# Log decays of the DeltaNet heads: products of fp32 numbers in two ranges of tiles, in place of four split float32r sets

## The chip, the cores and the metric

The kernel runs on one core of a Trainium2 chip. The metric is the device time of one execution in microseconds (us). Each core has a matrix engine (TensorE, in the rows PE for the products and PEld for the loading of their weights), a vector engine (VectorE, DVE), an engine for activation functions (ScalarE, ACT), GpSimd (POOL) and a queue engine (SyncE, SP) that issues most transfers. Every engine takes its instructions in a fixed order.

## What is computed

One layer of a diffusion backbone over 256 context tokens and 512 latent tokens of width 1024. A token mixer with two groups of four heads (HGRN2, a gated linear recurrence, and gated DeltaNet), both run forward and backward, is followed by a mixture of 16 experts. The change is in the DeltaNet heads. The reference, cut to what matters for it:

```python
def gated_delta_chunk_scan(q, k, v, beta, log_a, s0):
    ...
    cum = jnp.cumsum(log_a.astype(jnp.float32).reshape(b, h, n, DN_CHUNK), axis=-1)
    ...
    diff = cum[..., :, None] - cum[..., None, :]
    decay = jnp.where(incl, jnp.exp(jnp.where(incl, diff, 0.0)), 0.0)
    kk = jnp.einsum('bhntd,bhnsd->bhnts', kn, kn).astype(jnp.float32)
    a_mat = jnp.where(strict, bn[..., :, None] * kk * decay, 0.0) + jnp.eye(DN_CHUNK, dtype=jnp.float32)
    ...
    sol = lax.linalg.triangular_solve(a_mat, rhs, left_side=True, lower=True, unit_diagonal=True)
    ...
    qk = jnp.einsum('bhntd,bhnsd->bhnts', qn, kn) * decay.astype(dt)
    ...
```

`log_a` is one number for a token, a head and a direction. `decay[t, s]` is the exponential of the sum of the log decays of the tokens after s up to t. The lower triangle of a tile belongs to the forward direction and the upper one to the backward direction.

## The kernel before

The 768 tokens stand in NT = 6 tiles of 128. The kernel takes the sums of log decays from TensorE. For a head `h`, `dn_decay(h)` (L594) writes a tile of masks scaled by the log decay of each token (`seg`, tokens in partitions) and multiplies it with a constant triangle, so that entry (s, t) of the product is the sum of the log decays between s and t. One direction uses the masks `le` and `gt`, the other `ge` and `lt`; both add up into the same PSUM tile. ScalarE then takes the exponential (`E`), scales it by `beta` for either direction (`EB` and the scratch tile `bm`, L621), and VectorE puts the two triangles together (L622, COPY_PREDICATED). `E` and `EB` go to `dn_prep`: the products `pkk` (keys with keys, L668) are scaled by `EB`, and `pqk` (L675) by `E`. `dn_inv` inverts the 128x128 triangles by blocks, a long series of short steps on VectorE, ScalarE and TensorE, and writes `UF` and `UB`. `dn_scan` then runs over the six tiles, with `pks`, `px`, `po` and `pS` on TensorE between steps on VectorE and ScalarE.

Before the change the log decays `la` were split into a part `lah` that float32r holds and the rest `lal` (L513 to L515). The triangles had float32r copies (`gtr`, `ltr`, L518 and L519). For a head there are thus four sets (two directions, two parts). A set is six scalings on ScalarE (L612) and two products (L614), one of 256 columns into `pe{h}_0` and one of 512 columns into `pe{h}_2`. Each PSUM tile is complete only after the last of the four sets, and the two exponentials (L617) come after that. The buffer of `seg` exists once, so a set waits until the products of the set before have read it; the scratch tile `bm` uses the same buffer.

`dn_decay(0)` and `dn_decay(1)` are called ahead of the loop over heads; inside it `dn_decay(h + 2)` stands between the inverse of head `h + 1` and the HGRN2 head `h`. What fills TensorE meanwhile are the projections: `proj_cm` (L459 and L465: `hq0pl`, `hf_0pl`, `hf_1pl`, `dq1pl`, ..., for HGRN2 and DeltaNet), `proj_tm` (L859: values `hi0p`, gates `z10p`), each with a split of the raw weights (cast on ScalarE L393, e.g. `hq00h`, rest on VectorE L394, `hq00l`). The convolution over `qc`, `kc`, `vc` takes most of VectorE's time early on. The order in which each engine gets its instructions is decided by a scheduler with its own cost model when the program is built, and only nudged by priorities in the code; so a change in one function moves instructions of others. In the mixture of experts, each expert is a series of products `pg`, `pu` (L1546), `at`, `xt`, `py` (L1584) over weights that arrive by transfers and are split on ScalarE and VectorE.

## Time and profile before

| | us |
|---|---|
| three runs | 950.5, 952.97, 954.2 |
| median | 952.97 |
| profiled execution: time, span of the core | 949.7, 947.9 |
| mean granted TensorE clock of the profiled execution | 0.977 |
| busy in the span: PE, PEld, DVE, ACT | 876.5, 715.5, 711.0, 548.0 |

The span runs from the first to the last instruction of the core; 1.8 us of the execution's time lie around it. A busy time is the sum over the records of an engine; where two records overlap they count once. The granted clock is 1.00 at 2.4 GHz and 0.50 at 1.2 GHz.

### The profile page before, as it was taken

To read this page: it belongs to the slowest core of one execution; us is meant where nothing else is said; L and a number is where in the kernel's file an instruction comes from. 1 tells how busy PE (TensorE), PEld (TensorE's weight loads), DVE (VectorE), ACT (ScalarE), POOL (GpSimd) and SP (SyncE) were. 2 spreads that over 40 slices of the span, in tenths; PEclk is the share of its full clock that TensorE was granted. 3 is DMA by queue.
4 is the path that set the end of the run, shared out by engine and by line. 5 is a ranking of instruction groups with operands and counts; after the bars stand their busy time and mean duration, and the time that the engine had idled before them with its cause. 6 is when DMAs were issued, how large, how long until landed. Compare 5 with 4: busy or idle time off the path is not lost. (4 is left out here: it accounts for less than half of the span.)

```text
span 947.9 us, 20548 instructions
## 1 busy us (share of the span) xinstructions
PE 876.5 (92%) x8221; PEld 715.5 (75%) x8221; DVE 711.0 (75%) x1438; ACT 548.0 (58%) x1127; POOL 95.8 (10%) x106
## 2 busy tenths in 40 slices
PE   2999998979989999899998989899999999999994
PEld 1678887868878887787886968757888887777772
DVE  2687479745897679865585655868989988888986
ACT  4347753485258634932533333137888888788762
POOL 3231100000010000100000010111111111010011
PEclk9999998999979999999999989999999999999998
DMA  9920711200102111138219187669999999999745
GB/s 315 314 65 18 252 52 41 69 23 24 47 24 57 35 45 27 35 104 268 90 50 298 57 277 282 211 229 388 371 371 370 361 371 375 374 363 377 285 138 141
DMA packets 116237, 179.91 MB, mean 190 GB/s; under 512 B 10023, under 2 KB 49251, under 8 KB 116008
## 3 DMA queue, kind: packets, MB, share of 16 engines
q1 hardware_dynamic: 109272, 163.49, 50.7%
q0 software_dynamic: 6544, 14.71, 4.6%
q8 instruction: 66, 1.08, 0.5%
q10 hardware_dynamic: 320, 0.34, 0.1%
q14 instruction: 35, 0.29, 0.1%
HBM read 170.18 MB, written 16.27 MB: 197 GB/s over the span
## 5 line engine op out<-in xcount | busy, mean ns | idle before, releaser
L1422 DVE TENSOR_TENSOR lo<-w,hi 128x1024 fp32r<-128x1024 f32 x184 | 216.7, 1221 | 26.8 <-ACT hi L1417 25.0
L1417 ACT CAST hi<-w 128x1024 fp32r<-128x1024 f32 x184 | 186.0, 1050 | 21.7 <-PE pu L1546 9.6
L1584 PE MATMUL py<-lo,ah 128*128 128x512 f32 x128 | 51.6, 403 | 0.7
L1584 PE MATMUL py<-hi,ah 128*128 128x512 f32 x128 | 50.5, 396 | 0.0
L1584 PE MATMUL py<-hi,al 128*128 128x512 f32 x128 | 49.4, 396 | 0.3 <-DVE al L1576 0.3
L1546 PE MATMUL pg<-lo,xh 128*128 128x512 f32 x120 | 48.6, 405 | 0.0
L1546 PE MATMUL pu<-lo,xh 128*128 128x512 f32 x120 | 48.2, 402 | 0.2 <-DVE lo L1422 0.2
L1546 PE MATMUL pg<-hi,xh 128*128 128x512 f32 x120 | 47.5, 396 | 0.0
L1546 PE MATMUL pu<-hi,xl 128*128 128x512 f32 x120 | 47.4, 395 | 0.0
L1546 PE MATMUL pu<-hi,xh 128*128 128x512 f32 x120 | 47.4, 395 | 0.0
L1546 PE MATMUL pg<-hi,xl 128*128 128x512 f32 x120 | 47.4, 395 | 0.0
L1402 POOL DMA_INDIRECT y_d<-y,cl x15 | 17.6, 1173 | 132.9 <-ACT y L1588 119.7
L1584 PEld LDWEIGHTS py<-lo,ah 128*128 128x128 f32 x128 | 24.0, 188 | 8.7 <-DVE lo L1422 3.4
L941 DVE TENSOR_TENSOR KS<-KS,F 128x384 f32<-128x384 f32 x56 | 28.7, 553 | 2.1 <-ACT km L904 1.5
L1395 POOL DMA_INDIRECT xg<-t_d,cl x15 | 18.4, 1226 | 115.5 <-PE xt L1534 111.2
L814 DVE TENSOR_SCALAR vs<-px,bs 128x128 f32<-128x128 f32 x48 | 16.7, 348 | 16.8 <-PE px L812 16.4
L1584 PEld LDWEIGHTS py<-hi,ah 128*128 128x128 f32 x128 | 24.0, 188 | 6.4 <-ACT ah L1575 0.6
L1584 PEld LDWEIGHTS py<-hi,al 128*128 128x128 f32 x128 | 24.0, 188 | 6.1 <-DVE al L1576 0.8
L1546 PEld LDWEIGHTS pu<-lo,xh 128*128 128x128 f32 x120 | 22.5, 188 | 8.0 <-DVE lo L1422 2.9
L1006 PE MATMUL psm<-wm,cl 128*32 128x128 f32 x512 | 24.0, 280 | 4.9 <-DMA wm<-in_w_mod_dram 4.8
L1546 PEld LDWEIGHTS pu<-hi,xh 128*128 128x128 f32 x120 | 22.5, 188 | 5.4
L1546 PEld LDWEIGHTS pg<-hi,xh 128*128 128x128 f32 x120 | 22.5, 188 | 5.4
(1065 smaller groups left out, 2641.2 us busy)
## 6 DMA issues: line engine op xcount, KB each, us to landing
w<-in_w_gate_dram SPq DMA_DIRECT2D x32, 1024.0 KB, 16.0
w<-in_w_up_dram SPq DMA_DIRECT2D x32, 1024.0 KB, 15.0
w<-in_w_down_dram SPq DMA_DIRECT2D x32, 1024.0 KB, 15.2
wm<-in_w_mod_dram SPq DMA_DIRECT2D x64, 256.0 KB, 4.0
wm<-in_w_mod_dram SPq DMA_DIRECT2D x16, 512.0 KB, 8.5
y_d<-zt POOLq DMA_DIRECT2D x8, 512.0 KB, 6.9
wor<-in_w_out_dram SPq DMA_DIRECT2D x7, 512.0 KB, 4.9
xt<-in_x_dram SPq DMA_DIRECT2D x4, 512.0 KB, 11.7
```

The costliest lines, as they stand in the source:

```text
L814: nc.vector.tensor_scalar(vs, px[:, 0:P], bs[:, d, i:i + 1], None, op0=ALU.mult)
L941: nc.vector.tensor_mul(kh, kh, tt(d, 1 - d))
L1006: nc.tensor.matmul(ps[32 * c_:32 * c_ + 32, P * j:P * j + P], cl[:, kb, :], raw[:, P * c_:P * c_ + P], start=(kb == 0), stop=(kb == KB - 1))
L1395: return nc.gpsimd.indirect_dma_start(out=dst, out_offset=None, in_=t_d[:, :], in_offset=bass.IndirectOffsetOnAxis(ap=idx, axis=0), bounds ...
L1402: i_ = nc.gpsimd.indirect_dma_start(out=y_d[:, :], out_offset=bass.IndirectOffsetOnAxis(ap=idx, axis=0), in_=src, in_offset=None, bounds_c ...
L1417: nc.scalar.copy(hi, raw)
L1422: s.append(lo_on.tensor_sub(s[1], raw, s[0].bitcast(F32)))
L1546: a_pu[0] = nc.tensor.matmul(ps, m[:, kb, :], ww[:, k, :], start=(kb == 0 and n == 0), stop=(kb == KB - 1 and n == 2))
L1584: mm = nc.tensor.matmul(ps, m[:, k, :], ww[:, k % 2, :], start=(k == 0 and n == 0), stop=(k == 3 and n == 2))
```

## The change

The split of `la` and the float32r copies of the triangles go. The six tiles are worked in two ranges of three. A range has its own PSUM tile and its own `seg` tile (three tiles by two directions), six scalings of the unsplit `la`, six fp32 products of 128 columns straight with the constant triangles, and one exponential of 384 columns. The scalings by `beta` and the merge of the triangles stay as they were. In the new program the lines stand 10 lower before `dn_decay` and 13 lower after it: scalings L602, products L603, exponential L604, scalings by `beta` L608, merge L609.

```diff
-    lah = cp.tile([P, NT, 8], F32, name="lah")
-    lal = cp.tile([P, NT, 8], F32, name="lal")
-    lahr = grr[:, 256:256 + NT * 8].rearrange("p (i n) -> p i n", i=NT)
-    nc.vector.tensor_copy(lahr, la)
-    nc.vector.tensor_copy(lah, lahr.bitcast(F32))
-    nc.vector.tensor_sub(lal, la, lah)
-    gtr = cp.tile([P, P], F32R, name="gtr")
-    ltr = cp.tile([P, P], F32R, name="ltr")
-    nc.vector.tensor_copy(gtr, K("gt"))
-    nc.vector.tensor_copy(ltr, K("lt"))
...
-        rng = ((0, 2), (2, 4))
-        pe = [psI(f"pe{h}_{t0}") for t0, n in rng]
-        for d, m in ((0, "le"), (1, "ge")):
-            for a, l in ((0, lah), (1, lal)):
-                seg = dn.tile([P, NT, P], F32R, tag="seg", name=f"seg{h}_{d}_{a}")
-                for i in range(NT):
-                    nc.scalar.mul(seg[:, i, :], K(m), l[:, i, 4 * d + h:4 * d + h + 1])
-                for j, (t0, n) in enumerate(rng):
-                    nc.tensor.matmul(pe[j][:, 0:n * P], (gtr, ltr)[d], seg[:, t0:t0 + n, :],
-                                     start=(d == 0 and a == 0), stop=(d == 1 and a == 1))
-        for j, (t0, n) in enumerate(rng):
-            nc.scalar.activation(E[:, t0:t0 + n, :], pe[j][:, 0:n * P].rearrange("p (i t) -> p i t", i=n), AF.Exp)
+        n = NT // 2
+        for t0 in (0, n):
+            pe = psI(f"pe{h}_{t0}")
+            seg = dn.tile([P, n, 2, P], F32, tag="seg", name=f"seg{h}_{t0}")
+            for i in range(n):
+                for d, m in enumerate(("le", "ge")):
+                    nc.scalar.mul(seg[:, i, d, :], K(m), la[:, t0 + i, 4 * d + h:4 * d + h + 1])
+                    nc.tensor.matmul(pe[:, i * P:(i + 1) * P], K(("gt", "lt")[d]), seg[:, i, d, :], start=(d == 0), stop=(d == 1))
+            nc.scalar.activation(E[:, t0:t0 + n, :], pe[:, 0:n * P].rearrange("p (i t) -> p i t", i=n), AF.Exp)
```

The order on ScalarE around the decays of head 0, before. Between the second pair of sets and the exponentials stand the sigmoids of the HGRN2 projection `hf_0` (`F`, `KS`) and two casts of weights for DeltaNet head 1 (`dk10h`, `dk11h`); the row `ACT_TABLE_LOAD` fetches the table of another function.

```order
L874 ACTIVATE F_1049<-hf_0pl 128x512
L874 ACTIVATE KS_1048<-hf_0pl 128x512
L612 ACTIVATE seg_1_1_721<-cst,lal 128x128 x6
L393 CAST dk10h<-dk1r_1664 128x512
L393 CAST dk11h<-dk1r_1670 128x512
L875 ACTIVATE F_1049<-hf_0pc 128x256
L875 ACTIVATE KS_1048<-hf_0pc 128x256
L617 ACT_TABLE_LOAD
L617 ACTIVATE E_690<-pe_0_692 128x256
L621 ACTIVATE EB_691<-E_690,beta 128x128 x2
L617 ACTIVATE E_690<-pe_2_693 128x512
```

The same engine now, from the copy of the query projection `dq0pl` into the padded tile on. Before, that copy stood 13 rows ahead of the piece above.

```order
L544 COPY lpad_659<-dq0pl 128x8x64
L604 ACT_TABLE_LOAD
L604 ACTIVATE E_681<-pe_0_683 128x384
L602 ACTIVATE seg_3_699<-cst,la 128x128 x6
L608 ACTIVATE EB_682<-E_681,beta 128x128 x3
L974 COPY vp_846<-hi0p_975 128x256
L393 CAST hq00h<-hq0r_1031 128x512
L393 CAST hq01h<-hq0r_1037 128x512
L624 COPY kt_778<-pk_0_782 128x256
L604 ACTIVATE E_681<-pe_3_698 128x384
```

The exponentials have moved ahead of the casts `hq00h` and `hq01h`, which stood right behind that copy, and ahead of all sigmoids of `hf_0`.

The order on TensorE where head 0 is scanned (`px`, `pS`, `pks`) and the decays of head 1 are taken, before:

```order
L614 MATMUL pe_2_1608<-seg_0_0_1609,gtr 128x512
L834 MATMUL pS_0_0_1879<-vs_0_0_1877,kd_0_0_1880 128x128
L812 MATMUL px_0_1_1884<-vt_798,UB_674 128x128
L970 MATMUL hpk_3_0_2812<-cst,KS_1048 128x128
L614 MATMUL pe_0_1607<-seg_0_1_1618,gtr 128x256
L834 MATMUL pS_0_1_1888<-vs_0_1_1886,kd_0_1_1889 128x128
L807 MATMUL pks_1_0_1893<-S_0_1873,kc_746 128x128
L614 MATMUL pe_2_1608<-seg_0_1_1618,gtr 128x512
L974 MATMUL hpS_3_0_2816<-vp_865,kst_3_0_2814 128x128
```

And now:

```order
L603 MATMUL pe_3_1603<-seg_3_1604,cst 128x128
L623 MATMUL pk_0_2044<-cst,kc_1632 128x128 x2
L603 MATMUL pe_3_1603<-seg_3_1604,cst 128x128
L821 MATMUL pS_0_0_1850<-vs_0_0_1848,kd_0_0_1851 128x128
L799 MATMUL px_0_1_1855<-vt_779,UB_665 128x128
L603 MATMUL pe_3_1603<-seg_3_1604,cst 128x128 x4
L459 MATMUL hq1pl<-hlo,hq11h 128x512
L961 MATMUL hpS_2_0_2753<-vp_846,kst_2_0_2751 128x128
L949 MATMUL hpo_2_1_2757<-vp_846,hatt_2707 128x128
```

Before, no projection stood among the first steps of this scan. Now the projection `hq1pl` of HGRN2 head 1 runs between them. Further on in the new order, the inverse of head 1 and the scan that follows it have a stretch of about 150 TensorE entries without a projection.

## Rows read from the trace of the kernel before

**Rows 1.** The page, part 1: busy time, share of the span, records.

```profile
PE 876.5 (92%) x8221; PEld 715.5 (75%) x8221; DVE 711.0 (75%) x1438; ACT 548.0 (58%) x1127; POOL 95.8 (10%) x106
```

**Rows 2.** Busy time by stretch; last columns granted clock, DMA share, GB/s.

```profile
75.00:550.00 475.00, 447.39 (x6097) 380.57 (x6096) 338.61 (x893) 254.29 (x734) 24.00 (x28) 0.98 0.27 83
98.00:114.00 16.00, 16.00 (x95) 14.06 (x93) 4.12 (x7) 12.64 (x35) 0.22 (x1) 1.00 0.86 303
130.00:180.00 50.00, 45.12 (x825) 39.44 (x824) 49.23 (x122) 19.64 (x48) 0.00 (x0) 0.93 0.17 42
140.00:160.00 20.00, 15.62 (x342) 13.22 (x344) 19.96 (x51) 5.11 (x11) 0.00 (x0) 0.83 0.21 54
192.70:213.10 20.40, 15.47 (x96) 11.66 (x92) 10.22 (x30) 18.62 (x58) 0.00 (x0) 1.00 0.10 27
250.00:280.00 30.00, 26.19 (x592) 20.61 (x592) 29.55 (x88) 14.85 (x50) 2.51 (x2) 0.83 0.11 29
370.00:400.00 30.00, 24.40 (x175) 20.46 (x174) 27.43 (x66) 27.07 (x92) 3.46 (x3) 0.94 0.12 36
677.33:695.45 18.12, 18.12 (x86) 14.81 (x85) 16.46 (x17) 15.50 (x18) 2.77 (x2) 1.00 1.04 363
817.24:835.95 18.71, 18.58 (x85) 14.58 (x85) 16.39 (x17) 15.04 (x18) 2.02 (x2) 1.00 1.04 368
```

**Rows 3.** Groups by line and shape on ACT: busy, mean ns | idle before, releaser.

```profile
L612 ACT ACTIVATE seg<-cst,lah 128x128 fp32r<-128x128 f32 x48 | 15.3, 401 | 1.6 <-DVE lah L514 1.6
L612 ACT ACTIVATE seg<-cst,lal 128x128 fp32r<-128x128 f32 x48 | 15.1, 389 | 1.3 <-PE pe L614 1.3
L617 ACT ACT_TABLE_LOAD x4 | 5.1, 1283 | 0.1
```

**Rows 4.** Timeline of PE: start, length, instruction, [idle before, releaser].

```profile
94.56 0.28 PE L614 MATMUL pe<-seg,gtr 128*128 128x256 f32 x1
94.67 0.39 PE L459 MATMUL hq0pl<-hhi,hq01l 128*128 128x512 f32 x1
...
96.96 0.39 PE L614 MATMUL pe<-seg,gtr 128*128 128x512 f32 x1
97.19 0.40 PE L459 MATMUL hf_0pl<-hhi,hf_00h 128*128 128x512 f32 x1
...
133.21 1.06 PE L668 MATMUL pkk<-kc 128*128 128x128 f32 x8
134.20 0.34 PE L910 MATMUL pa<-QP,km 128*32 128x32 f32 x16
134.46 1.16 PE L675 MATMUL pqk<-qc,kc 128*128 128x128 f32 x8
135.55 0.34 PE L910 MATMUL pa<-QP,km 128*32 128x32 f32 x16
```

**Rows 5.** Timeline of ACT, decays of head 0.

```profile
81.88 1.87 ACT L612 ACTIVATE seg<-cst,lah 128x128 fp32r<-128x128 f32 x6 [1.61 <-DVE lah L514]
...
88.32 0.59 ACT L554 COPY lpad<-dq0pl 128x512 f32<-128x512 f32 x1 [0.76 <-DVE vc L576]
...
107.01 0.36 ACT L875 ACTIVATE KS<-hf_0pc 128x256 f32<-128x256 f32 x1
107.40 1.28 ACT L617 ACT_TABLE_LOAD   x1
108.69 0.39 ACT L617 ACTIVATE E<-pe 128x256 f32<-128x256 f32 x1
```

**Rows 6.** Timeline of DVE: the merge of head 0.

```profile
114.11 1.03 DVE L622 COPY_PREDICATED EB<-cst,bm 128x768 f32<-128x768 int32 x1 [6.47 <-ACT bm L621]
```

**Rows 7.** Timeline of PE: three of its waits.

```profile
91.66 0.50 PE L459 MATMUL hq0pl<-hhi,hq00l 128*128 128x512 f32 x1 [0.74 <-DVE hq00l L394]
...
213.13 0.50 PE L459 MATMUL hf_1pl<-hhi,hf_10h 128*128 128x512 f32 x1 [1.75 <-ACT KS L874]
...
375.14 0.47 PE L614 MATMUL pe<-seg,gtr 128*128 128x512 f32 x1 [1.75 <-DVE UB L791]
```

## The prediction

> **What bounds the kernel now.** I began with the busy times of the page [rows 1]. TensorE is busy for 92% of the span and no other engine for more than 75%. A mean over the whole program hides the stages, so I cut the span into stretches [rows 2]. In the mixer, from 75 to 550 us, TensorE is busy for 447.4 of 475 us. Of the 27.6 us in which it is not, I looked for the stretches that hold most, and for what the other engines do there. The reader should see four kinds of place:
>
> - 98 to 114 us: TensorE is full (16.00 of 16 us) and VectorE is almost empty (4.12 us). The merge of head 0's decays ends that emptiness; it starts at 114.11 us, after VectorE waited 6.47 us for ScalarE [rows 6].
> - 130 to 180 us: VectorE is full (49.23 of 50 us) with head 0's inverse and scan, the HGRN2 head and the convolutions of head 1. TensorE idles 4.9 us, and its granted clock is 0.93. The core of it is 140 to 160 us: 4.4 us idle and a clock of 0.83, so part of it ran at 1.2 GHz.
> - 192.7 to 213.1 us: the scan of head 0 beside the decays of head 1, with no projection but one product. TensorE is busy for 15.47 of 20.4 us, ScalarE for 18.62 us.
> - 250 to 280 us and 370 to 400 us, the same for heads 2 and 3: TensorE idles 3.8 and 5.6 us; VectorE is busy 29.55 and 27.43 of 30 us; ScalarE is at 14.85 and 27.07 us.
>
> So the mixer is bound by TensorE, with holes where chains of short steps lack something to fill them. The decays lie ahead of the inverse, which opens these chains. In the experts, TensorE is full or nearly so (18.12 of 18.12 us, 18.58 of 18.71 us [rows 2]).
>
> **TensorE: what the change adds.** Removed are 4 heads x 4 sets x 2 products: 16 of 256 columns and 16 of 512. What one takes is the distance from its start to the next: 94.67 - 94.56 = 0.11 us and 97.19 - 96.96 = 0.23 us [rows 4]; together 16 x 0.34 = 5.4 us. Added are 4 x 12 = 48 fp32 products of 128 columns. The nearest rows are `pkk` and `pqk`, fp32 products of the same shape: four in 134.20 - 133.21 = 0.99 us, and four in 135.55 - 134.46 = 1.09 us (eight records, two for one product) [rows 4]. That is 0.25 to 0.27 us each, 11.9 to 13.1 us in all. TensorE gets 6.5 to 7.7 us more; I take 6.9, or 1.7 for a head. Heads 1 and 3 have their decays in stretches where TensorE idles, and pay little. For heads 0 and 2 TensorE is full around them, and I count all of it: **+3.4**. If the cover at heads 1 and 3 is gone, it is 6.9.
>
> **ScalarE: what it loses.** 96 scalings become 48. A run of six takes 1.87 us [rows 5], so one costs 0.31 us and not the 0.40 us of the group's mean [rows 3], in which neighbours overlap. 48 x 0.31 = 14.9 us. Exponentials are eight before and after, over the same columns: nothing. The new order has 21 table loads instead of 19, since the two exponentials of head 1 have other functions between them: 2 x 1.28 [rows 3] = 2.6 us. Net ScalarE has 12.3 us less.
>
> A table load takes 1.28 us, and around the one at 107.40 us the neighbours follow at once: KS ends at 107.37, the exponential begins at 108.69 [rows 5]. The Trainium skill ("ScalarE: Activation LUTs", "What ACT_TABLE_LOAD costs") gives a drain of about 1.38 us on top, 2.66 us for each switch; by it the two loads would cost 5.3 us of ScalarE instead of 2.6. In this trace no such gap stands.
>
> **VectorE** loses five copies and subtractions on small tiles. They lie between operations of the convolution. Only one is seen to be waited for: the first `seg` waited 1.61 us for `lah` [rows 5]. I count nothing for it, since TensorE has the projection `hi0p` at that time; at most it is a gain of 1.6 us.
>
> **Head 0: the decays come earlier.** In the new order the first exponential stands right behind the copy of `dq0pl`, which ends at 88.32 + 0.59 = 88.9 us [rows 5]. With its table load it starts at about 90.2, against 108.69. The second six scalings end at about 92.6, their products about 1 us later, and the second exponential at about 95. Twelve scalings by `beta` (12 x 0.31 = 3.7 us), the casts and a few squares of head 0's keys that stand between them bring the merge to about 101 us, 13 us earlier than 114.1 [rows 6]. It moves into the stretch in which VectorE has 12 of 16 us free [rows 2]. Then the scaling by `EB` and the inverse begin earlier, and 130 to 180 us, where VectorE is full, is relieved of part of them. What is there to win is the idle 4.9 us and the clock: 0.17 x 20 = 3.4 us of granted cycles from 140 to 160 us. That makes 8.3 at most. VectorE's work itself does not shrink, so the other end is nothing. I take **-5**, nearer the full end since 13 us are more than the hole is long.
>
> The cost of it: the cast `hq00h` stood right behind that copy and now stands behind a table load, an exponential (0.5 us), six scalings (1.87) and three by `beta`: about 4.7 us later. TensorE already waited 0.74 us for its rest `hq00l` [rows 7]. It now has the longer products of both ranges ahead (counted above) and transposes of keys and values, about 4 us, so the new wait would be 0.5 to 2.5 us, with the products of the second range pacing behind their scalings. I take **+1.5**.
>
> **Head 1: 192.7 to 213.1 us.** ScalarE is at 18.62 of 20.4 us. Twelve scalings fewer free 3.7 us, two more table loads take 2.6 back. The decays of head 1 now lie among products of `hq1pl`, which can run while a step waits, where before no projection stood. To win are 4.9 us by the busy time of TensorE. In the new order, though, a later piece (inverse of head 1 and the next scan) has lost its projections, and may idle in its place. I take **-3**, between 0 and -4.9.
>
> The weight loads are busy for only 11.66 us in that stretch [rows 2], so by them there are 8.7 us of room. The Trainium skill ("Perfetto Trace Analysis", "Identifying the Most-Contended Engine") holds that matmul busy time is a poor measure of headroom and points to the weight loads instead. By it the term could reach -8.7, and the sum would be up to 5.7 us lower. The trace has no row that decides this.
>
> **Heads 2 and 3.** The decays of head 2 lie beside a VectorE that is full (29.55 of 30 us): shorter scalings on a ScalarE with 14.85 us of work free nobody directly. Idle time there is 3.8 us; I take **-2**. At head 3 ScalarE is busy 27.07 of 30 us, and TensorE idles 5.6 us; a product waits 1.75 us there for the inverse [rows 7]. 3.7 us of ScalarE go: **-3.5**, between 0 and -5.6.
>
> **The experts.** They come in two forms, of 18.12 and 18.71 us [rows 2]; the second has a wait for a split weight in it. Six experts have the second order before, four in the new one: 2 x 0.6 = **-1.2**. The transfers of weights wait for buffers that the splits free, so I let the experts shift with the end of the mixer.
>
> **Sum.** 3.4 + 1.5 - 5 - 3 - 2 - 3.5 - 1.2 = -9.8 us against the profiled execution's 949.7: 939.9. That execution lies 3.3 us under the median of 952.97, so the median would be 943.2; I say **943.5**. With gains at their full ends (8.3 + 4.9 + 3.8 + 5.6 + 1.2 = 23.8) and costs at the low ones (3.4 + 0.5) it is -19.9: 933. With no gain and all costs (7.7 + 2.5) it is +10.2: 963.
>
> **Rivals.** A measurement of this kernel can tell about 0.5%, or 4.8 us, from no change; that puts "no change" at 948.2 to 957.7.
>
> *Holes only move.* VectorE's chain, not ScalarE, sets the length of the holes (49.23 of 50 and 29.55 of 30 us busy). Earlier decays let projections be used up earlier, and the next scan lacks them: the stretch without projections in the new order speaks for it. Against it: VectorE's free 12 us at 98 to 114 us are real room. The gains would be about 6 us instead of 14.7, against 4.9 of costs: -1, some 952.
>
> *TensorE pays (slower).* A kernel that is 92% TensorE gets 6.9 us more work for it, and relief of an engine at 58% is worth nothing. It needs head 1 and head 3 to lose their cover, and the waits at `hq00l` in full: 6.9 + 2.5 = 9.4 us. It ends slower by over 0.5% as soon as less than 9.4 - 4.8 = 4.6 us of holes are closed; with 2 us it is +7.4, or 960.
>
> *All holes close.* If head 0's start 13 us earlier takes the whole chain of heads along, the full gains stand: 933 to 936. Against it speaks that the chain of VectorE has as much work as before.
>
> **How the numbers follow.** My forecast 0.56 (937 to 950; some 0.07 of it above 948.2), all holes close 0.08, holes only move 0.20 (948 to 955, with 0.02 past either edge), TensorE pays 0.16. Faster: 0.49 + 0.08 + 0.02 = 0.59. Same: 0.07 + 0.16 = 0.23. Slower: 0.16 + 0.02 = 0.18. The range 931 to 960 leaves out half of the slower case and the edge of the fastest. The forecast's own range is 937 to 950.
>
> **What would show it.** Right: the first exponential of head 0 at about 90 us and its merge near 101; a TensorE group of 48 fp32 products at 0.25 to 0.27 us of pace; ScalarE's total down by about 12 us; less idle time and a clock near 1.00 at 140 to 160 us; four experts of the longer form. Wrong: the wait for `hq00l` over 3 us; a new hole of more than 5 us in the inverse of head 1 or the next scan; the end of the mixer no earlier although the merge is; products of the new form above 0.3 us, or at half clock, since they come in runs behind waits.

## The result and the profile after

The change makes the kernel faster by about 1%: 942.63 us median of four runs (939.4 to 945.5) against 952.75 us of four runs of the kernel before (950.5 to 954.2), a ratio of 0.9896 with a 95% interval of 0.9873 to 0.9920. The forecast was 943.5. The total came out as forecast, in part by luck: two effects behind the mixer that no term of mine had, one of about 5 us and one of 4 to 6 us, have opposite signs. Not all of the terms came out either. The experiments below show both.

First the page of the kernel after, part 1, and its groups for the lines of the change (these answer to [rows 1] and [rows 3]):

```profile
PE 868.5 (92%) x8285; PEld 719.7 (77%) x8285; DVE 712.9 (76%) x1433; ACT 536.4 (57%) x1081; POOL 99.2 (11%) x106
```

```profile
L602 ACT ACTIVATE seg<-cst,la 128x128 f32<-128x128 f32 x48 | 15.0, 391 | 2.4 <-DVE EB L609 1.6 <-DVE la L509 0.8
L604 ACT ACT_TABLE_LOAD x5 | 6.4, 1283 | 0.1
L604 ACT ACTIVATE E<-pe 128x384 f32<-128x384 f32 x8 | 3.9, 489 | 0.9 <-PE pe L603 0.9
```

ScalarE is busy 11.6 us less (548.0 to 536.4); I had worked out 12.3. TensorE is busy 8 us less (876.5 to 868.5) although it was given more products; where that comes from is said below (the clock, and the pace of the experts).

The decays of head 0, on ScalarE, VectorE and TensorE (compare [rows 5], [rows 6] and the first of [rows 7]):

```profile
86.57 0.59 ACT L544 COPY lpad<-dq0pl 128x512 f32<-128x512 f32 x1 [0.76 <-DVE vc L566]
87.18 1.28 ACT L604 ACT_TABLE_LOAD   x1
88.47 0.49 ACT L604 ACTIVATE E<-pe 128x384 f32<-128x384 f32 x1
88.86 1.85 ACT L602 ACTIVATE seg<-cst,la 128x128 f32<-128x128 f32 x6
...
91.75 0.62 ACT L393 CAST hq00h<-hq0r 128x512 fp32r<-128x512 f32 x1
```

```profile
97.90 1.09 DVE L609 COPY_PREDICATED EB<-cst,bm 128x768 f32<-128x768 int32 x1 [1.36 <-ACT bm L608]
```

```profile
84.41 1.50 PE L603 MATMUL pe<-seg,cst 128*128 128x128 f32 x12
85.67 0.36 PE L846 MATMUL hi0p<-hi01l,hhi 128*128 128x256 f32 x1
...
93.84 0.48 PE L459 MATMUL hq0pl<-hhi,hq00l 128*128 128x512 f32 x1
```

The first exponential starts at 88.5 us instead of 108.7, the merge at 97.9 instead of 114.1, and the first product with `hq00l` at 93.84 instead of 91.66. The idle time of 0.74 us that stood before this product [rows 7] is gone: its row has none.

The stretches (columns as in [rows 2]; the first row here is the kernel before, from 75 us to the first product of the output projection, `mt`, which ends the mixer; the other rows are of after):

```profile
75.00:539.00 464.00, 436.39 (x6037) 371.36 (x6036) 329.38 (x875) 245.68 (x710) 22.95 (x27) 0.98 0.27 80
```

```profile
75.00:527.60 452.60, 431.60 (x6098) 373.17 (x6097) 330.17 (x870) 234.73 (x664) 25.56 (x27) 0.99 0.28 82
140.00:160.00 20.00, 18.26 (x428) 15.68 (x419) 20.00 (x53) 8.26 (x20) 0.00 (x0) 1.00 0.22 56
192.70:213.10 20.40, 18.43 (x346) 15.90 (x346) 15.62 (x56) 9.97 (x37) 1.33 (x1) 1.00 0.10 27
169.00:187.00 18.00, 18.00 (x137) 16.14 (x136) 12.56 (x23) 16.74 (x43) 0.00 (x0) 1.00 0.28 74
250.00:280.00 30.00, 26.04 (x226) 21.96 (x225) 28.54 (x77) 20.88 (x73) 3.98 (x3) 0.94 0.14 36
360.00:390.00 30.00, 25.88 (x311) 23.91 (x310) 25.48 (x62) 23.31 (x71) 5.92 (x3) 0.89 0.15 44
713.10:730.90 17.80, 17.80 (x86) 14.79 (x85) 16.42 (x17) 15.39 (x19) 2.84 (x2) 1.00 1.01 380
```

From 140 to 160 us the idle time fell from 4.4 to 1.7 us and the granted clock rose from 0.83 to 1.00. A stretch is the same time in both kernels, not always the same work. The decays of head 1, whose products stood at 192.8 to 202.6 us, now have theirs at 171.7 to 179.9 us, and TensorE does not idle around them (18.00 of 18 us busy). What stands at 192.7 to 213.1 us now idles for 2.0 us, where it was 4.9. Around 250 to 280 us a hole is still there (4.0 us idle, clock 0.94), and so is one at 360 to 390 us, where the decays of head 3 lie (4.1 us idle, clock 0.89). The mixer ends 11.5 us earlier (`mt` at 527.58 us, before at 539.04), with 21.0 us of idle time in place of 27.6. The clock adds to it: some 0.02 x 464 = 9 us of granted cycles missing before, 0.01 x 453 = 5 us now.

Two things happen behind the mixer that no term of mine had. An expert runs in 17.80 us where the same sequence of products took 18.12 before [rows 2]. And some of the 11.5 us are lost at once at the first expert. Timeline of after there, TensorE, then ScalarE, then SyncE's queue:

```profile
629.07 1.09 PE L1521 MATMUL xt<-cst,xg 128*128 128x128 f32 x8 [2.93 <-DMA xg<-t_d,cl]
634.88 1.11 PE L1554 MATMUL at<-cst,a 128*128 128x128 f32 x4 [4.72 <-DVE a L1545]
```

```profile
632.22 1.28 ACT L1544 ACT_TABLE_LOAD   x1 [14.61 <-SPq L1448]
```

```profile
618.44 1.23 SPq L1206 DMA_DIRECT2D w<-in_w_gate_dram  x2
621.03 0.37 SPq L1206 DMA_DIRECT2D w<-in_w_down_dram  x1
632.59 0.38 SPq L1206 DMA_DIRECT2D w<-in_w_up_dram  x1
```

L1448 is the branch on the overflow of experts. ScalarE comes to it early, then stands until SyncE's queue is done there, and only then takes the first expert's activation `a`, for which the transposes `at` wait. The instructions of the two queues at that line (count, ns, first and last start):

```profile
L1448 ACTq COMPARE_BRANCH  x1: 45/45/45, 614.0 to 614.0; - x1
L1448 SPq COMPARE_BRANCH  x1: 50/50/50, 621.4 to 621.4; - x1
L1448 SPq EVENT_SEMAPHORE  x8: 17/17/17, 626.9 to 632.1; - x8
```

In the kernel before, the last to come there was TensorE's own queue:

```profile
637.98 1.28 ACT L1557 ACT_TABLE_LOAD   x1 [10.56 <-PEq L1461]
```

The new order has four loads of weights ahead of the branch on SyncE's queue instead of two. In the trace three of them stand between the reading of the count and the branch (the SyncE rows above up to 621.03 us), where the kernel before has one. SyncE takes its compare at 621.4 us, so it is not the wait for free buffers that holds it. It then waits at the branch for each of its transfers: in the trace the second of the three loads has landed at 629.09 us and the third at 631.75, and SyncE's waits for these two end at 629.11 and 631.77. In the kernel before the one load has landed at 635.22 us and SyncE is through at 635.8, ahead of TensorE's queue. TensorE then starts the next expert after a pause in which its clock falls; from 634.9 to 643.5 us it is full but granted 0.68 (products 0.43 us apart at first, 0.23 later):

```profile
634.90:643.50 8.60, 8.60 (x29) 7.01 (x30) 4.40 (x6) 3.92 (x5) 0.00 (x0) 0.68 0.99 358
```

So `at` is only 5.8 us earlier than before (640.65 to 634.88), and the end of the program 7.9 us in the profiled executions (947.9 and 940.0 us).

### The profile page after: what moved, and what is told of

Read it like the earlier page. It is cut to its first block, busy times and chain, and to the rows that moved or that the text cites. A ratio compares the mean times of both kernels' runs of the same rounds, so it can differ in the third digit from the quotient of the medians.

```text
span 940.0 us, 20633 instructions
## 1 busy us (share of the span) xinstructions
PE 868.5 (92%) x8285; PEld 719.7 (77%) x8285; DVE 712.9 (76%) x1433; ACT 536.4 (57%) x1081; POOL 99.2 (11%) x106
## 5 line engine op out<-in xcount | busy, mean ns | idle before, releaser
L1031 POOL TENSOR_TENSOR nss<-nss,half 128x4 f32<-128x4 f32 x8 | 10.6, 1326 | 202.0 <-DVE nss L1028 125.2
```

The lines of the kernel that those rows point to most:

```text
L1031: nc.gpsimd.tensor_tensor(ss, ss, half[:, 0:NLT], op=ALU.pow)
```

## The experiments

Twelve kernels were run. A table first. "Mixer's end" is the start of `mt`; idle and clock of TensorE are those of the stretch from 75 us to it; the merge is that of head 0; all from one profile each. The median and the ratio are of the timed runs against the kernel before on the same chip.

| kernel | median us | ratio, 95% interval | mixer's end | idle | clock | merge |
|---|---|---|---|---|---|---|
| before | 952.75 | | 539.0 | 27.6 | 0.98 | 114.1 |
| the change | 942.63 | 0.9896, 0.9873 to 0.9920 | 527.6 | 21.0 | 0.99 | 97.9 |
| fp32_old_layout | 951.37 | 0.9987, 0.9962 to 1.0011 | 540.3 | 28.6 | 0.97 | 105.3 |
| split_two_ranges | 958.94 | 1.0064, 1.0035 to 1.0092 | 547.6 | 34.2 | 0.96 | 110.8 |
| new_head0 | 949.45 | 0.9974, 0.9950 to 0.9998 | 535.5 | 24.7 | 0.98 | 97.6 |
| new_heads123 | 959.64 | 1.0105, 1.0053 to 1.0157 | 548.4 | 33.3 | 0.96 | 113.0 |
| before_head0_four_tiles | 954.26 | 1.0031, 1.0013 to 1.0048 | 542.6 | 34.1 | 0.97 | 102.2 |
| after_head0_late | 940.89 | 0.9898, 0.9867 to 0.9928 | 533.8 | 23.5 | 0.97 | 101.7 |
| after_two_loads_ahead | 937.23 | 0.9855, 0.9828 to 0.9881 | 526.5 | 20.2 | 0.99 | 97.1 |
| after_double_scalings | 962.18 | 1.0093, 1.0061 to 1.0124 | 550.8 | 31.8 | 0.96 | 106.9 |
| after_tiles_moved_back | 948.45 | 0.9992, 0.9961 to 1.0022 | 527.8 | 21.0 | 0.99 | 98.0 |
| after_tiles_512_up | 943.09 | 0.9913, 0.9884 to 0.9942 | 528.8 | 22.8 | 0.99 | 98.2 |
| after_products_twice | 942.16 | 0.9904, 0.9876 to 0.9932 | 531.7 | 15.4 | 0.99 | 99.5 |
| before_directions_swapped | 953.56 | 1.0010, 0.9988 to 1.0032 | 545.4 | 29.5 | 0.97 | 115.3 |

Four kernels of the table (the change, two loads, moved back, 512 up) have the same order in the mixer. Their mixers end at 526.5 to 528.8 us, so these four profiles agree within 2.3 us. That is no bound for one profile: the executions of one kernel spread further (the kernel before from 949.0 to 959.6 us in 25 runs), and some profiles are of a short or a long one.

The totals also hold what comes behind the mixer, and there the kernels are of two kinds. In the change, fp32_old_layout, after_double_scalings, after_products_twice and the two with moved tiles, three loads stand between the count and the branch; in the others it is one. And an expert takes 17.8 us where the four removed tiles are gone (moved back excepted), 18.1 us where they are kept. So the mixer's end says more on the decays than the median does.

**fp32_old_layout: the new products, without the two ranges.**

```diff
+        for d, m in ((0, "le"), (1, "ge")):
+            seg = dn.tile([P, NT, P], F32, tag="seg", name=f"seg{h}_{d}")
+            for i in range(NT):
+                nc.scalar.mul(seg[:, i, :], K(m), la[:, i, 4 * d + h:4 * d + h + 1])
+            for j, (t0, n) in enumerate(rng):
+                nc.tensor.matmul(pe[j][:, 0:n * P], K(("gt", "lt")[d]), seg[:, t0:t0 + n, :], start=(d == 0), stop=(d == 1))
...
```

> The fp32 products and the halved scalings of the change, but in the layout of before: one set of six scalings for a direction over all six tiles, products of 256 and 512 columns, both exponentials only after the second set. Theory (my prediction's): the gain comes from decays that are ready earlier and from ScalarE's lighter load around them; ScalarE's part stays, the early exponential of the first three tiles goes, so some two thirds of the change's gain of 10 us, 944 to 948 us, and a merge of head 0 some 5 us later than with the change. Rival 1 (the split into two ranges does it): 951 to 955. Rival 2 (it is only where the fillers happen to be put): anything between 940 and 960, without relation to the merge of head 0.

Measured 951.4 us, no measurable gain. ScalarE has the lighter load (237.8 us to the mixer's end, before 245.7), and the merge of head 0 is 9 us earlier than before; but the mixer ends no earlier, although the hole at 140 to 160 us is closed. Halved scalings and the unsplit product together are worth nothing that can be seen in this layout.

```profile
75.00:540.30 465.30, 436.75 (x6034) 371.73 (x6033) 330.77 (x871) 237.80 (x666) 23.98 (x27) 0.97 0.27 80
140.00:160.00 20.00, 19.45 (x486) 17.01 (x474) 19.96 (x51) 6.73 (x15) 0.00 (x0) 1.00 0.22 56
```

**split_two_ranges: the two ranges, without the new products.**

```diff
+        for t0 in (0, n):
...
+            for d, m in ((0, "le"), (1, "ge")):
...
+                for a, l in ((0, lah), (1, lal)):
+                    for i in range(n):
+                        nc.scalar.mul(seg[:, a, i, :], K(m), l[:, t0 + i, 4 * d + h:4 * d + h + 1])
+                    nc.tensor.matmul(pe[:, 0:n * P], (gtr, ltr)[d], seg[:, a], start=(d == 0 and a == 0), stop=(d == 1 and a == 1))
```

> The two ranges of three tiles of the change, but with split float32r sets as before: 96 scalings, 32 products of 384 columns, no more work for TensorE than before. Theory (earlier decays and lighter ScalarE): the first range is ready after 12 scalings instead of 24, but ScalarE keeps its load: a small gain, 948 to 952 us. Rival 1 (the two ranges do it): the gain of the change plus the TensorE time that is not added, 937 to 943. Rival 2 (fillers by chance): 940 to 960.

Measured 958.9 us, slower than before. The merge of head 0 is only 3 us earlier than before, and the hole of the kernel before is still there:

```profile
140.00:160.00 20.00, 15.53 (x383) 12.76 (x384) 19.96 (x50) 5.10 (x11) 0.00 (x0) 0.83 0.22 55
```

With the former run it makes a square. Mixer's end: split sets in the old layout 539.0, fp32 in the old layout 540.3, split in two ranges 547.6, fp32 in two ranges 527.6 us. Each half alone gives nothing or costs 9 us; both together give 11.5.

**new_head0 and new_heads123: the change at some heads only.** Both keep the split parts and the old sets for the other heads.

```diff
+        if h == 0:
+            n = NT // 2
+            for t0 in (0, n):
...
+        else:
+            rng = ((0, 2), (2, 4))
...
```

In the second the condition is `h > 0`.

> The change at head 0 alone, heads 1 to 3 with split sets as before. My prediction's terms for it: +1.7 for products, +1.5 for the later cast, -5 for the earlier inverse, so -1.8 us: 951 us, with the hole at 140 to 160 us smaller. From the trace of the changed kernel, where the same work stands 1.5 us later at 110 us, 8 us earlier at 160 and 2 us earlier at 190, the same. Rival (head 0's start 13 us earlier takes the whole chain along): -6 to -10, 943 to 947. Rival (fillers by chance): 946 to 960.

> The change at heads 1 to 3, head 0 with split sets as before. My prediction's terms: -3 at head 1, -2 + 1.7 at head 2, -3.5 at head 3: -6.8 us, 946 us, if the heads' gains add up, and if the order of the experts stays that of before. Rival (TensorE pays where its cover is gone: 3 x 1.7 us): 955 to 958. Rival (fillers by chance): the two part runs do not add up to the whole, by more than 5 us.

Head 0 alone: 949.5 us, -2.5; my terms for head 0 gave -1.8. Heads 1 to 3 alone: 959.6 us, +7.7, where my terms gave -6.8. The parts add up to +5, the whole is -10 (at the mixer's end -3.5 and +9.3 against -11.5). What a head's new decays are worth depends on what the others did to the order. The rows of new_heads123 show where it loses: from the end of head 0's scan into head 1's, and where the scan of head 2 begins and the decays of head 3 end. The clock falls there too (in the kernel before, the same times have 4.0 and 3.3 us of idle time and clocks of 0.90 and 1.00):

```profile
250.00:300.00 50.00, 42.93 (x576) 37.73 (x575) 41.33 (x107) 31.64 (x104) 3.63 (x3) 0.83 0.09 23
380.00:410.00 30.00, 23.91 (x166) 22.06 (x166) 24.05 (x55) 21.13 (x63) 2.91 (x3) 0.89 0.09 27
```

**before_head0_four_tiles: early decays at head 0 by another way.**

```diff
-                seg = dn.tile([P, NT, P], F32R, tag="seg", name=f"seg{h}_{d}_{a}")
+                tag = ("seg", "vt", "kt", "vt")[2 * d + a] if h == 0 else "seg"
+                seg = dn.tile([P, NT, P], F32R, tag=tag, name=f"seg{h}_{d}_{a}", bufs=1 if tag == "seg" else 2)
```

> The kernel before, with one thing changed: at head 0 the four split sets take four tiles (three of them borrowed from buffers that are idle then), so that no set waits for the products of the set before. No new form of product, no lighter ScalarE. In the new order the first exponential of head 0 stands ahead of the casts of the HGRN2 weights, as with the change. Theory (the gain comes from head 0's decays being ready early, by whatever way): merge of head 0 near 100 us instead of 114, and a gain like that of the change at head 0 alone (-2.5 us there): 947 to 951. If moreover the early start of the scan is what the whole change lives on: 940 to 946. Rival (it is the unsplit products and the halved scalings): no gain, 951 to 955.

Measured 954.3 us: no gain, though the merge is at 102.2 us. The rows show that the mechanism worked and what it cost:

```profile
85.00:100.00 15.00, 9.93 (x55) 8.83 (x54) 5.64 (x10) 14.82 (x35) 2.57 (x5) 0.77 0.06 18
140.00:160.00 20.00, 18.47 (x449) 15.46 (x447) 20.00 (x52) 7.33 (x15) 0.00 (x0) 1.00 0.27 69
```

The hole at 140 to 160 us is closed (1.5 us idle, clock 1.00). But all 24 scalings now stand in one piece ahead of the work that feeds TensorE, which idles 5.1 of 15 us with a clock of 0.77 (before: 1.0 us and 1.00). With half as many scalings the change has its early merge without this price. The early merge does close the hole; that it carries the whole gain is refuted.

The whole table bears out both. In the ten kernels whose merge comes at 106.9 us or earlier, the clock at 140 to 160 us is 1.00 and the idle time at most 2.2 us; in the four with a merge at 110.8 us or later it is 0.83 and at least 4.4 us. But among the ten is after_double_scalings, the slowest kernel of all:

```profile
140.00:160.00 20.00, 19.97 (x456) 17.11 (x454) 20.00 (x53) 7.25 (x15) 0.00 (x0) 1.00 0.28 71
```

**after_head0_late: the change, with head 0's exponentials later.**

```diff
+            if h == 0:
+                tc.add_manual_dep(ex_.ins, conv_end[2].ins.name, later, reason="after the convolution")
...
-    dec[0] = dn_decay(0)
     with tc.issue_after(last_hi.ins):
         proj[0] = dn_proj(0)
+    dec[0] = dn_decay(0)
```

(`conv_end[2]` is the last step of the convolution of the queries. Unlike what the expectation says, one thing more is edited: the call of the decays of head 0 moves behind that of its projections.)

> The changed kernel, with the exponentials of head 0 put behind the convolution of the queries in the order, so that the merge of head 0 comes some 6 to 8 us later than with the change; nothing else is edited. Theory (head 0's early merge carries the gain): the gain is mostly lost, 948 to 954 us, and the hole at 140 to 160 us comes back. Rival (unsplit products and halved scalings in all heads): 941 to 945.

Measured 940.9 us, as fast as the change. The edit moved the merge by 3.8 us only, less than expected, and the hole at 140 to 160 us did not come back (1.5 us idle, clock 1.00), so it is a weak test. The mixer does end 6.2 us later than the change's, 533.8 us. The time is made good behind it: in this order only one load of weights stands between the count and the branch, and `at` follows 1.69 us after TensorE is free:

```profile
634.35 0.66 PE L1558 MATMUL at<-cst,a 128*128 128x128 f32 x4 [1.69 <-DVE a L1549]
```

So this total says less on head 0 than on the branch, which the next run tests. Against that run, which has one load there too, this kernel is 3.7 us slower.

**after_two_loads_ahead: the change, with two loads ahead of the branch.**

```diff
     order += [(NE - 1, 4), (NE - 1, 5)]
+    order[NR1 + NR2 + 1:NR1 + NR2 + 3] = order[NR1 + NR2 + 2], order[NR1 + NR2 + 1]
...
+    turns = turns[:NR1 + NR2] + "mom" + turns[NR1 + NR2 + 3:]
...
-    for i in range(4):
+    for i in range(2):
         load_weights()
```

(The first two edits exchange two of the loads, with their buffers.)

> The changed kernel, with two loads of expert weights ahead of the branch on the overflow of experts instead of four (the load of w_1, whose buffer waits for the products of the first expert, comes behind the branch, as it did before the change). The mixer's order is that of the changed kernel, row for row. Theory: with the change SyncE came late to the branch since it waited there for the first expert's products, and TensorE stood for 8.8 us between the first expert's products and the next instead of 3; without that 5 to 8 us less: 935 to 938. Rival (the gathers of tokens or the load of code set this stretch): within 2 us of 942.6. Open: the experts ran at 17.79 us each with the four loads ahead and at 18.11 with two; if that belongs to the loads, 4 us of it go back: 939 to 942.

Measured 937.2 us, 5.4 below the change (5.0 if each is taken against the kernel before on its own chip) and 15 below the kernel before; it beats both. The pause is gone, and so is the slow clock behind it (1.00 from 624.5 to 644 us):

```profile
627.37 0.65 PE L1557 MATMUL at<-cst,a 128*128 128x128 f32 x4 [1.52 <-DVE a L1548]
```

```profile
624.70 1.28 ACT L1547 ACT_TABLE_LOAD   x1 [8.77 <-PEq L1451]
```

```profile
624.50:644.00 19.50, 17.73 (x87) 14.71 (x88) 14.36 (x15) 16.19 (x20) 4.03 (x4) 1.00 0.99 374
```

The last to come to the branch is TensorE's queue again. SyncE has one load there now, which has landed at 623.24 us, and SyncE is through at 623.7. That confirms that the loads ahead of the branch made the pause; the reason in the expectation does not hold. SyncE waits 11.6 us for the first expert's products in both kernels, ahead of the first of these loads, and 0.4 us for them at the second with the change. What held it was the landing of the loads. The experts kept their 17.8 us, so the loads are not what sets that pace.

**after_tiles_moved_back and after_tiles_512_up: other addresses, same order.**

```diff
+    pad = cp.tile([P, 352], F32, name="pad")
     pcu = psI("pcu")
```

In the second the tile has 128 columns. Nothing uses it.

> The changed kernel with one more tile of 1408 bytes in each partition that nothing writes or reads, at the place where the removed tiles (the two parts of the log decays and the float32r triangles) stood. The order of all engines is that of the changed kernel, row for row; only the addresses of the tiles above it go back to those of the kernel before, among them the split weights of the experts. Theory (the experts run at 17.79 us in place of 18.11 since the weights stand at other addresses): experts at 18.11 us again, products of one expert 0.233 us apart instead of 0.229, and the time 4 to 5 us longer than the change's: 946 to 948. Rival (the order of the loads or of the program sets the pace): 942 to 944 and 17.79 us.

> The same with a tile of 512 bytes: the split weights of the experts then start at 73,728 bytes instead of 73,216 (the change) or 74,624 (before). If what counts is that they start at a multiple of 512 bytes, as with the change, the experts stay at 17.79 us: 942 to 944. If each shift gives a pace of its own, something else, up to 18.11 us: 942 to 948.

Moved back: 948.5 us in the median of ten runs (945.7 to 956.5); 512 up: 943.1. With the tiles moved back the ratio to the kernel before is 0.9992 (0.9961 to 1.0022): without the new addresses no gain of the change can be told in these totals, although its mixer ends 11.2 us earlier than before. The mixers are as with the change; the expert between the same two instructions takes:

```profile
732.80:750.90 18.10, 18.10 (x86) 14.72 (x85) 16.46 (x17) 15.49 (x19) 2.78 (x2) 1.00 1.03 370
```

moved back, and 512 up:

```profile
732.50:750.30 17.80, 17.80 (x86) 14.79 (x85) 16.41 (x17) 15.40 (x19) 2.82 (x2) 1.00 1.04 385
```

The addresses alone move the pace, by some 4 us in the program. Apart from the moved-back one, the kernels of this study without the four removed tiles all ran at 17.8 us; those with them ran at 18.1.

**after_double_scalings: the change, with ScalarE's load given back.**

```diff
-                    nc.scalar.mul(seg[:, i, d, :], K(m), la[:, t0 + i, 4 * d + h:4 * d + h + 1])
+                    for _ in range(2):
+                        nc.scalar.mul(seg[:, i, d, :], K(m), la[:, t0 + i, 4 * d + h:4 * d + h + 1])
```

> The changed kernel with each scaling of the masks done twice (the second time over the first, the same numbers): ScalarE has the load of before again, 96 scalings, the rest is the change. Theory of my prediction (ScalarE's lighter load helps at heads 1 and 3): 4 to 8 us of the gain go, 947 to 951. Rival (only the place of head 0's exponentials counts; they come some 2 to 4 us later): 943 to 947. Rival (where fillers happen to be put): 940 to 960, with the loss in other places than around the decays.

Measured 962.2 us: 19.5 more than the change, for 48 scalings of 0.31 us, 15 us of an engine that is busy for 57% of the span. None of the expectations reached that far. The order moved as well, since the scheduler sees more work: about half of TensorE's entries up to `mt` stand in the sequence of the change, so the run does not separate ScalarE's load from the new order. It agrees with split_two_ranges, the other kernel with two ranges and 96 scalings: their mixers end at 550.8 and 547.6 us, with 48 scalings at 527.6. The mixer's end moved by 23.2 us, with 10.8 us more idle time; the clock of 0.96 (0.99 with the change) makes 0.03 x 476 = 14 us of granted cycles. The loss is spread over the heads, as at head 0 and from the end of head 2's scan on:

```profile
85.00:105.00 20.00, 17.04 (x102) 15.10 (x101) 11.36 (x18) 19.11 (x44) 6.25 (x9) 0.91 0.33 114
...
430.00:480.00 50.00, 48.13 (x861) 36.90 (x862) 25.22 (x76) 17.38 (x53) 4.41 (x6) 0.90 0.56 174
```

**after_products_twice: the change, with TensorE's added work doubled.**

```diff
-                    nc.tensor.matmul(pe[:, i * P:(i + 1) * P], K(("gt", "lt")[d]), seg[:, i, d, :], start=(d == 0), stop=(d == 1))
+                    for r in range(2):
+                        nc.tensor.matmul(pe[:, i * P:(i + 1) * P], K(("gt", "lt")[d]), seg[:, i, d, :], start=(d == 0 and r == 0), stop=(d == 1 and r == 1))
```

> The changed kernel with each fp32 product of the decays done once more, into columns of the PSUM tile that nothing reads: 48 products of 128 columns more, 11.9 to 13.1 us of TensorE by the pace of such products, ScalarE and VectorE as with the change. Rival of my prediction (TensorE pays for each product): 12 to 13 us longer, 954 to 956. My prediction's cover (heads 1 and 3 hide theirs, heads 0 and 2 pay): 6 to 7 us longer, 948 to 950. The order moves too, since the scheduler sees longer products: if that decides, 940 to 962, with the difference in other places than the products.

Unlike what the expectation says, the second product goes into the columns of the first and adds up with it. So this kernel takes the exponential of twice the sums and computes other numbers; only its time is read. Measured 942.2 us, the same as the change. By the pace in the profile after (six products in 85.67 - 84.41 = 1.26 us) 48 more are 10 us. The mixer ends 4.1 us later, and idle time falls from 21.0 to 15.4 us: more than half of the new products fill holes. Here too only about half of TensorE's entries keep the sequence of the change, so the run shows what such products cost in an order made for them.

```profile
75.00:531.70 456.70, 441.32 (x6201) 382.93 (x6201) 330.98 (x873) 238.16 (x669) 24.31 (x27) 0.99 0.27 82
```

**before_directions_swapped: a change without content.**

```diff
-        for d, m in ((0, "le"), (1, "ge")):
+        for d, m in ((1, "ge"), (0, "le")):
```

(with the start and stop flags exchanged)

> The kernel before with the two directions of the decays in the other order (backward set first): the same number of every instruction and the same result. The order of ScalarE and VectorE stays, TensorE's differs in places up to the middle of the mixer. If small moves of fillers matter little: within 3 us of before, 950 to 955. If they are worth as much as the change: 942 to 962.

Measured 953.6 us, no change. Its profiled execution was the longest of its ten runs (956.6), so the mixer's end of 545.4 us is above what is usual for it. Against the kernel before on its chip (952.05) the medians are 1.5 us apart, and the interval is -1 to +3 us. So this small move, which leaves nearly all of TensorE's entries in their sequence, is not worth 10 us. It says nothing on moves as large as those of the change or of the runs above.

## Why the prediction was right, point by point

**Head 0, the early merge: right in mechanism and place; its worth at the end is smaller.** The first exponential was forecast near 90.2 us and came at 88.5; the merge near 101, and it came at 97.9. The hole at 140 to 160 us gave what was there (2.7 us of idle time and 3.4 us of clock), and in all fourteen kernels this hole goes with the merge. The cost at `hq00l` is 2.2 us of delay, most of it the longer products ahead of it; the new wait of 0.5 to 2.5 us that I forecast there did not come, and the old one of 0.74 us went. Around the table load the neighbours follow at once, as before: it ends at 88.46, the exponential begins at 88.47. The drain of 1.38 us that the Trainium skill ("ScalarE: Activation LUTs", "What ACT_TABLE_LOAD costs") adds is not in this trace either. For head 0 in all I had -1.8, the run with head 0 alone -2.5 (-3.5 at the mixer's end). That is less than the 6.1 us that the hole itself gave back. The run with four tiles shows the limit: a merge nearly as early, bought with 24 scalings in one piece, cost 4 us of idle time and 3 us of clock at once and brought nothing.

**TensorE's price: right that most is hidden, mis-sized on the safe side.** I took half of the 6.9 us as paid. Ten more microseconds of such products, in an order made for them, moved the mixer's end by 4.1 and the time by nothing that can be measured. The products themselves are cheaper than `pkk` and `pqk` made them (0.25 to 0.27 us): six take 1.26 us from the first to the next instruction, 0.21 each, so that TensorE got 48 x 0.21 - 5.4 = 4.7 us more and not 6.9. One sign that I had named for being wrong did come: the first six products of head 3 ran at half clock behind waits of TensorE, at 0.45 us each:

```profile
369.64 2.93 PE L603 MATMUL pe<-seg,cst 128*128 128x128 f32 x12
372.36 0.64 PE L799 MATMUL px<-vt,UF 128*128 128x128 f32 x2
```

```profile
369.60:372.30 2.70, 2.70 (x16) 2.66 (x13) 2.64 (x6) 1.38 (x3) 0.00 (x0) 0.50 0.39 97
```

That adds 1.5 us to the 4.7. The rival that TensorE pays falls with the total: it gave 960.

**ScalarE: this is the step whose size the runs contradict.** I let the lighter ScalarE count only where it looked full, at heads 1 and 3, and wrote that it frees nobody directly at head 2. The kernel with the 48 scalings given back, in its own order, took 19.5 us more, and the rows show that idle time and low clock make up that loss. In the layout of before the same 48 scalings were worth nothing that can be seen (fp32_old_layout). My reading, which no run shows by itself: the scalings stand ahead of every inverse, so a head that gets its decays later meets other fillers. The rival, that the scheduler merely made a worse order there, is not excluded: no run has the scalings doubled in the order of the change.

**Heads 1 to 3 as terms that add up: failed.** I summed -3, -0.3 (gain and products at head 2) and -3.5. At head 1 the idle time of the stretch fell by 2.9 us, as I had it. At head 2 I had misread the stretch: the decays of head 2 do not lie at 250 to 280 us, where the inverse of head 1 runs, but later, in a stretch that hardly idles (280 to 300 us: 0.1 us).

```profile
L614 PE MATMUL pe<-seg,gtr x4: 364/429/505, 283.4 to 290.4; 128*128 128x256 f32 x2, 128*128 128x512 f32 x2
```

At head 3 idle time and low clock stayed (4.1 us and 0.89 at 360 to 390 us now, 5.6 us and 0.94 at 370 to 400 us before), so of the -3.5 little is seen. On their own, heads 1 to 3 cost 7.7 us; with head 0 done as well, they lead from 949.5 to 942.6, which is -6.8, the very sum I had (-7.9 at the mixer's end). That agreement is chance: the same terms were off by 14 us without head 0, and the totals differ by the branch and the experts as well. In the square of layout and products neither half gives anything alone. In a program whose order a scheduler decides, the trace of before tells where time can be won, but not that the wins are independent.

**The experts: failed.** I had -1.2 for the order of two experts and let the rest shift with the mixer. In the profiled executions the mixer won 11.5 us and the program 7.9. The branch cost 5.7 us up to `at` and some 3 more at low clock; the faster experts gave back about 4. Both are shown by runs: with the loads put back behind the branch the time falls by 5.4 us, and with the tiles at the old addresses it rises (by 3.9 us in the profiled spans, 940.0 to 943.9, and by 5.8 in the medians). That the two cancelled, so that the total hit 943.5 within 1 us, is luck. The order showed the two extra loads ahead of the branch; I had read them and not asked when they land.

**Holes only move** was half right: a hole at 250 to 280 us stayed, and the gain of head 0 alone at the mixer's end is 3.5 of 11.5 us. The new hole that I had feared there, of more than 5 us, did not come (4.0 us, where 3.8 stood). **All holes close** is refuted by 21.0 us of idle time.

Open: why heads 1 to 3 with head 0 in the old form lose 9 us at the mixer's end rather than merely win less. The rows show where (250 to 300 and 380 to 410 us), not which entry of the order is to blame. Open for the same reason is why the two halves of the change, the ranges and the fp32 products, gain only together; that the order falls well by chance is a rival that no run excludes.

## What to carry to other kernels

Where a scheduler sets the order, forecast a change as a range for the whole and test its parts together as well as apart: here the parts summed to +5 us and the whole was -10. A program with more short work on a half-idle engine can lose more than the length of that work (19.5 us for 15 here), in idle time and clock; how much of it is the work and how much the new order stayed open. A total that comes out as forecast is no proof of its terms: compare the end of the stage that was changed, too. When an order changes, look at which loads each queue now has ahead of a branch, since here the queue waited at the branch until they had landed. The two extra loads cost half as much as the whole change gained, and putting them back made the fastest kernel of the study.

## What the hardware showed that I had not expected

**Addresses change the pace of products.** With the order of all instructions unchanged, the products of the experts ran 0.233 us apart with the split weights at 74,624 bytes of a partition, and 0.229 us with them at 73,216 or 73,728. That is 0.3 us of 18 for an expert. The two fast places are multiples of 512 bytes and the slow one is not; three places do not prove that rule. The rows of the moved-back kernel (0.23 to 0.24 us apart):

```profile
711.13 0.39 PE L1535 MATMUL pg<-lo,xh 128*128 128x512 f32 x1
711.37 0.39 PE L1535 MATMUL pg<-hi,xl 128*128 128x512 f32 x1
...
712.77 0.39 PE L1535 MATMUL pg<-hi,xl 128*128 128x512 f32 x1
```

From the first to the last of these are seven steps in 1.64 us, 0.234 each; with two loads ahead of the branch, and the weights at the change's addresses, eight take 1.83 us, 0.229 each:

```profile
700.00 0.39 PE L1536 MATMUL pg<-hi,xh 128*128 128x512 f32 x1
...
701.83 0.39 PE L1536 MATMUL pg<-hi,xl 128*128 128x512 f32 x1
```

**The clock falls with the holes, though not in step with them.** Mixers that end at 526 to 532 us had a granted clock of 0.99, those that end at 547 us or later 0.96. Between them it does not follow the idle time: after_head0_late has 23.5 us of it and 0.97, the kernel before 27.6 us and 0.98. After the pause at the branch TensorE was full and granted 0.68 of 2.4 GHz for 8.6 us; without the pause it was granted 1.00 in the same place of the program.
